# One SwiGLU up step by plain block products, a fixed TensorE order at its entry, row norms on VectorE and deeper lookahead

## The chip, the cores and the metric

The kernel runs on one core of one Trainium2 chip. The metric is the device time of one execution in microseconds (us); smaller is better. All arithmetic is fp32. A matrix product of fp32 operands is made of three TensorE matmuls on "fp32r" halves: every operand is split into a high part (h) and a low part (l = x - h), and h·h, h·l and l·h are summed in PSUM.

## The reference, cut to what matters

One layer: a token mixer (attention beside a gated MLP), then the SwiGLU feed-forward part, each followed by a layer norm of the scaled residual. The change lies in the second half:

```
z   = layer_norm(alpha*x + g1 * mixer(x)) * ln1_g + ln1_b     # (1024, 1024)
h2  = z * (1 + scale) + shift                                 # adaLN modulation
a   = silu(h2 @ w1) * (h2 @ w3)                               # w1, w3: (1024, 2816)
out = layer_norm(alpha*z + g2 * (a @ w2)) * ln2_g + ln2_b     # w2: (2816, 1024)
```

## The kernel before, in words

Z holds the eight 128-row tiles of the normalised stream, h2 its modulated transpose. The first half (mixer, output projection, h2 of the rows 512 to 1023) is not touched by the diff beyond line numbers.

**Up.** `h2 @ w1` and `h2 @ w3` are done in 22 steps (p, w): p is one of 11 pairs of 128 columns of the feed-forward width, w=0 is w1 and w=1 is w3. In each step a 2x2 block product is made with 7 block products in place of 8 (a Strassen-Winograd scheme), 12 matmuls of 128x512 each (`prod`, L1093 to L1095). `up_first` makes A11·B11 (PSUM tile pa, copied to SBUF at L1138), `up_second` adds A12·B21 on pa. `up_rest` makes S2·T2 (tile pb, added to the copy at L1153), S1·T1 and S4·B22 (first half "c" of tile pcd), S3·T3 and A22·T4 (second half "d" of pcd). c is copied by ScalarE (L1161), added by GpSimd (L1165), and d and c are added by VectorE (L1169, L1174, L1177). The S are sums of weight blocks (`prep2`, L1070 to L1078, then split), the T are sums of h2 blocks made once by `make_h2b`: eight groups of four TensorE transposes of Z (tile pz, written by L128), an affine on ScalarE (L845, tiles h2X and h2H), subtractions and splits on VectorE. A split is a cast on ScalarE (L102, wH) and a subtraction on VectorE (L107, wL). `act_out` does the silu on ScalarE (w=0) and the product on VectorE (w=1, L1115) and sends activations to a DRAM tile combP. `w2_sums(p)` loads a block of w2, scales it on GpSimd (L1035), forms four sums on VectorE (tile wt) and sends these to combP too. Of the first NE=5 steps `up_first` and `up_second` run ahead, while the T are not there yet; they need B11 and B21 alone.

**Down.** `a @ w2` takes the products P1, P5, P6, P3, P2, P7, P4 in that order, each over the 11 p, 12 matmuls for each (L1292, PSUM tiles px and py). Operands are read back from combP (tile cr) and split (L102, L107) `prep_to` pairs ahead of TensorE. Between products VectorE adds PSUM to the rows R (L1239, L1365). Rows 4 to 7 are complete after P2 and are normalised by `norm_slow` while P7 runs: statistics (L1259, L1261, L123), the root on GpSimd (L124, L1268), scale on ScalarE (L1270), gain on VectorE (L1272), bias on GpSimd (L1274). Rows 0 to 3 are completed by P4 and go through `norm_fast` (L1282, L1284).

**Order.** Every engine runs its instructions in the order in which they stand. A recording layer fixes this order when the program is built, from the order of the code and its estimates; `order(a, b)` forces a behind b, and `at` puts a VectorE instruction behind the last recorded matmul. Dependencies are kept for whole tiles: the two halves of pcd count as one.

## Time and profile before

| | us |
|---|---|
| median of 3 runs (1256.88 to 1259.43) | 1257.02 |
| the profiled execution's own time | 1260.01 |
| its span in the profile | 1258.3 |
| TensorE (PE) busy | 1201.2 (95%) |
| VectorE (DVE) busy | 960.7 (76%) |
| ScalarE (ACT) busy | 563.3 (45%) |
| GpSimd (POOL) busy | 324.9 (26%) |

The span is the profiled stretch of that one execution; its own time includes 1.7 us around the span. Busy shares are means over stages: TensorE is at 95% over all, but stretches with gaps stand between stretches without any. The mean granted TensorE clock of the execution is 0.986 of full speed.

### The profile page before, as it was taken

Reading aid. Unit: us, or ns where it says so; the run is one execution under the profiler, and the core shown is the slowest. Engines: PE = TensorE matmul, PEld = TensorE weight load, DVE = VectorE, ACT = ScalarE, POOL = GpSimd, SP = SyncE. Lnnn points to the kernel's source line nnn. Section 1 sums busy time; section 2 is a strip of 40 time slices with the busy share of each in tenths; the row PEclk is TensorE's granted clock in tenths of the full one; section 3 lists DMA queues with packets and bytes.
Section 4 is the critical chain, followed back from the end, with each engine's and each line's share of the span. In section 5 each row is a group of like instructions: output and inputs, shape, how many; then the busy total and the mean of one; then the engine's idle time right before and its main releaser. Section 6 shows DMA issues by size and latency. Waiting matters only on the chain.

```text
span 1258.3 us, 16864 instructions
## 1 busy us (share of the span) xinstructions
PE 1201.2 (95%) x5884; PEld 998.5 (79%) x5884; DVE 960.7 (76%) x1682; ACT 563.3 (45%) x1033; POOL 324.9 (26%) x331
## 2 busy tenths in 40 slices
PE   7999999999999999999788999999999999999977
PEld 5888888788888888788566878888888877888865
DVE  6568798699999988776877766866767769864685
ACT  5644223499889993134412331332322323552440
POOL 0022045266456753100223202222122200000131
PEclk9999999999999999999889989999999999999989
DMA  9624549010000006542156655456565569893552
GB/s 355 232 67 122 169 138 239 28 68 1 1 2 1 2 19 234 184 131 96 47 179 209 192 164 173 157 184 192 170 190 177 160 224 347 274 302 106 194 181 83
DMA packets 131979, 188.60 MB, mean 150 GB/s; under 512 B 16819, under 2 KB 78387, under 8 KB 131894
## 3 DMA queue, kind: packets, MB, share of 16 engines
q1 hardware_dynamic: 131894, 187.52, 46.1%
q8 instruction: 46, 0.75, 0.3%
q14 instruction: 39, 0.32, 0.1%
HBM read 136.63 MB, written 48.76 MB: 147 GB/s over the span
## 4 chain that ended last, share of the span: by engine, by line
PE 79%; DVE 11%; DMA 4%; issue 3%; ACT 2%; POOL 1%; DVEq 0%; SPq 0%; ACTq 0%; POOLq 0%
PE py L1292 7%; PE px L1292 6%; PE pcd L1093 5%; PE pcd L1094 5%; PE pcd L1095 5%; PE pt L128 4%; PE pa L1093 3%; PE pa L1095 3%; PE pa L1094 3%; PE ps L730 2%; PE ps L732 2%; PE ot L774 2%; PE pwo L92 2%; PE pwo L96 2%; PE pwo L95 2%
## 5 line engine op out<-in xcount | busy, mean ns | idle before, releaser
L102 ACT ACTIVATE wH<-cr 128x1024 fp32r<-128x1024 f32 x77 | 80.8, 1059 | 104.7 <-DMA cr<-combP 95.1
L743 POOL TENSOR_SCALAR P<-P,ast,gate 128x640 f32<-128x640 f32 (+7 forms) x128 | 99.5, 783 | 66.5 <-DVE ast L742 42.2
L107 DVE TENSOR_TENSOR wL<-cr,wH 128x1024 fp32r<-128x1024 f32 x77 | 100.3, 1317 | 20.0 <-ACT wH L102 19.1
L1165 POOL TENSOR_TENSOR pt<-pt,pt 128x512 f32<-128x512 f32 x22 | 36.3, 1648 | 269.9 <-DVE pt L1153 181.4
L107 DVE TENSOR_TENSOR pt<-pt,pt 128x512 fp32r<-128x512 f32 (+1 forms) x148 | 99.9, 682 | 7.0 <-ACT pt L102 6.3
L676 ACT ACTIVATE P<-P,ast 128x640 f32<-128x640 f32 (+7 forms) x128 | 94.0, 736 | 2.0 <-DVE ast L675 1.5
L102 ACT ACTIVATE pt<-pt 128x512 fp32r<-128x512 f32 (+1 forms) x148 | 87.4, 593 | 16.1 <-PE pt L128 13.4
L1035 POOL TENSOR_TENSOR w2r<-w2r,g2r 128x512 f32<-128x512 f32 x44 | 62.8, 1448 | 72.0 <-DMA w2r<-in_w 60.4
L128 PE MATMUL pt<-ident,P 128*128 128x128 f32 x528 | 79.0, 272 | 0.2 <-DVE pt L107 0.2
L1292 PE MATMUL px<-wH 128*128 128x512 f32 x176 | 68.5, 396 | 9.1 <-DVE r L1239 6.8
L102 ACT ACTIVATE wH<-raw 128x1024 fp32r<-128x1024 f32 (+2 forms) x41 | 42.4, 1040 | 76.2 <-DMA combP<-wt 63.3
L128 PEld LDWEIGHTS pt<-ident,P 128*128 128x128 f32 x528 | 65.0, 140 | 12.9 <-issue 0.5
L1093 PE MATMUL pa<-h2H,wH 128*128 128x512 f32 x176 | 70.2, 400 | 4.2 <-ACT wH L102 3.5
L1095 PE MATMUL pa<-h2H,wL 128*128 128x512 f32 x176 | 69.6, 395 | 1.8 <-DVE wL L107 1.8
L1093 PE MATMUL pcd<-wH,wH 128*128 128x512 f32 x176 | 70.1, 398 | 1.1 <-ACT wH L102 0.7
L107 DVE TENSOR_TENSOR wL<-raw,wH 128x1024 fp32r<-128x1024 f32 (+2 forms) x41 | 49.0, 1198 | 28.6 <-ACT wH L102 22.9
L1094 PE MATMUL pcd<-wL,wH 128*128 128x512 f32 x176 | 69.8, 397 | 0.6 <-DVE wL L107 0.6
L1292 PE MATMUL px<-wL,wH 128*128 128x512 f32 x176 | 69.1, 393 | 1.0 <-DVE wL L107 1.0
L1094 PE MATMUL pa<-h2L,wH 128*128 128x512 f32 x176 | 69.9, 397 | 0.0
L1095 PE MATMUL pcd<-wH,wL 128*128 128x512 f32 x176 | 69.2, 393 | 0.0
L1292 PE MATMUL px<-wH,wL 128*128 128x512 f32 x176 | 69.0, 392 | 0.0
L773 PE MATMUL ot<-pt,V 128*128 128x512 f32 x132 | 59.7, 452 | 0.0
(298 smaller groups left out, 3500.8 us busy)
## 6 DMA issues: line engine op xcount, KB each, us to landing
cr<-combP SPq DMA_DIRECT2D x77, 512.0 KB, 4.8
raw<-in_w SPq DMA_DIRECT2D x49, 512.0 KB, 6.0
ada<-in_w_adaT SPq DMA_DIRECT2D x32, 512.0 KB, 6.8
w2r<-in_w SPq DMA_DIRECT2D x44, 256.0 KB, 3.0
combP<-wt SPq DMA_DIRECT2D x44, 256.0 KB, 5.5
combP<-as SPq DMA_DIRECT2D x44, 256.0 KB, 2.1
combP<-w2r SPq DMA_DIRECT2D x33, 256.0 KB, 2.0
ada<-in_w_ada SPq DMA_DIRECT2D x32, 256.0 KB, 3.7
```

Of the source, the lines that this page charges most:

```text
L102: A_.activation(o, i, AF.Copy)
L107: return V_.tensor_tensor(o, i, f(h), SUB)
L128: nc.tensor.transpose(out=p[:, j * 128:(j + 1) * 128], in_=src(j), identity=ident)
L676: A_.activation(P, P, AF.Exp, scale=-1.0, bias=nm, accum_out=den)
L743: P_.tensor_scalar(P, P, st[:, 2, hh:hh + 1], gcol(i, h, br), MULT, MULT)
L773: nc.tensor.matmul(ot, vs, hl[0], start=False, stop=False)
L1035: order(P_.tensor_tensor(r[z][a], r[z][a], rowt["g2r"][:, a * 512:a * 512 + 512], MULT), lasth[0])
L1093: nc.tensor.matmul(o, lh, rh, start=start and i == 0, stop=False, skip_group_check=not start)
L1094: nc.tensor.matmul(o, lh, rl, start=False, stop=False, skip_group_check=not start)
L1095: r = nc.tensor.matmul(o, ll, rh, start=False, stop=i == 3, skip_group_check=not start)
L1165: P_.tensor_tensor(p5, p5, p1, ADD)
L1292: lastm[0] = nc.tensor.matmul(o, x_[:, ts_], y_[:, 512:1024], start=not cont and p == 0 and n == 0, stop=p == NP - 1 and n == 2, skip_grou ...
```

## The change

1. The first up step (p=0, both w) is made by 8 plain block products in place of 7 (`classic`): A11·B11 + A12·B21 and its three sisters. It takes no S and no T, but a split B12, which `make_h2b` makes with B22. Two of the four plain outputs go on pa ahead of the T, the other two (on the halves of a pcd tile) after the two early `up_first`/`up_second` of the steps 2 and 3. NE becomes 4.
2. All early products and the transposes of Z are chained in their order of the code (`in_order`); a part of `make_h2b` is issued after the 13th, 16th, 19th and 22nd group of three matmuls (`TR`).
3. T1 to T4 are formed later and in another order, and the tie `lasth` that held `w2_sums` behind them is gone.
4. `w2_sums` of p=0, 1, 2 runs at the steps 3, 5, 4 and no longer at 0, 2, 4.
5. `up_rest` has one order for all steps (S4·B22 after S3·T3).
6. `norm_slow` has two VectorE instructions (subtract the mean and multiply by the gain; multiply by the root and add the bias) in place of the chain over GpSimd, ScalarE, VectorE and GpSimd.
7. `prep_to` looks up to 7 further pairs ahead from n=24 on, in place of up to 4 from n=40 on.

```diff
...
     def make_h2b():
 
         x12, x22, x11, x21 = [], [], X1P[0:2], X1P[2:4]
+
+        def place(n, j, t):
+            h, l = split(t)
+            BOP[n][2 * j:2 * j + 2] = zip(halves(h), halves(l))
         for i in range(4):
             if i % 2 == 0:
                 x12.append(B("h2X"))
...
                 bh, bl = B("h2H", F32R), B("h2L", F32R)
             for k, xx in ((i, x12[-1]), (4 + i, x22[-1])):
                 p = S2("pz")[:, 0, :]
-                trans4(p, lambda j: Z[j][:, k * 128:(k + 1) * 128])
+                for j in range(4):
+                    in_order(nc.tensor.transpose(out=p[:, j * 128:(j + 1) * 128], in_=Z[j][:, k * 128:(k + 1) * 128], identity=ident))
                 affine("A", halves(xx)[i % 2], p, k)
                 if k >= 4:
                     affine("A", halves(bh)[i % 2], p, k)
             if i % 2:
                 sub(bl, x22[-1], bh)
                 BOP["B22"][i - 1:i + 1] = zip(halves(bh), halves(bl))
-                t1 = x11[i // 2]
-                V_.tensor_tensor(t1, x12[-1], t1, SUB)
-                h, l = split(t1)
-                BOP["T1"][i - 1:i + 1] = zip(halves(h), halves(l))
+                place("B12", i // 2, x12[-1])
             yield
         spill_z(0)
-
-        def place(n, j, t):
-            h, l = split(t)
-            lasth[:] = lasts
-            BOP[n][2 * j:2 * j + 2] = zip(halves(h), halves(l))
         for j in range(2):
+            V_.tensor_tensor(x11[j], x12[j], x11[j], SUB)
+            place("T1", j, x11[j])
             V_.tensor_tensor(x11[j], x22[j], x11[j], SUB)
-            V_.tensor_tensor(x21[j], x21[j], x11[j], SUB)
             place("T2", j, x11[j])
             yield
         for j in range(2):
             V_.tensor_tensor(x12[j], x22[j], x12[j], SUB)
             place("T3", j, x12[j])
-            yield
-        for j in range(2):
+            V_.tensor_tensor(x21[j], x21[j], x11[j], SUB)
             place("T4", j, x21[j])
             yield
+
+    lastpe = []
+
+    def in_order(i):
+
+        if lastpe:
+            order(i, lastpe[0])
+        lastpe[:] = [i]
+        return i
 
     def advance_h2(n=1):
         for _ in range(n):
...
             load(r[z][0], w2[(2 * p + z) * 128:(2 * p + z + 1) * 128, 0:512], 8)
             load(r[z][1], w2[(2 * p + z) * 128:(2 * p + z + 1) * 128, 512:1024], 8)
             for a in range(2):
-                order(P_.tensor_tensor(r[z][a], r[z][a], rowt["g2r"][:, a * 512:a * 512 + 512], MULT), lasth[0])
+                P_.tensor_tensor(r[z][a], r[z][a], rowt["g2r"][:, a * 512:a * 512 + 512], MULT)
         (t1, t3), (t2, t4) = halves(B("wt")), halves(B("wt"))
         V_.tensor_tensor(t1, b12, b11, SUB)
         V_.tensor_tensor(t3, b22, b12, SUB)
...
         sub(l, a22, h)
         o["A22"] = pieces(h, l)
 
-    def prod(o, a, b, start=True):
+    ticks = [0]
+
+    def prod(o, a, b, start=True, early=False):
 
         for i in range(4):
             (lh, ll), (rh, rl) = a[i], b[i]
-            nc.tensor.matmul(o, lh, rh, start=start and i == 0, stop=False, skip_group_check=not start)
-            nc.tensor.matmul(o, lh, rl, start=False, stop=False, skip_group_check=not start)
-            r = nc.tensor.matmul(o, ll, rh, start=False, stop=i == 3, skip_group_check=not start)
+            for n, (x_, y_) in enumerate(((lh, rh), (lh, rl), (ll, rh))):
+                r = nc.tensor.matmul(o, x_, y_, start=start and i == 0 and n == 0, stop=i == 3 and n == 2, skip_group_check=not start)
+                if early:
+                    in_order(r)
+            if early:
+                ticks[0] += 1
+                if ticks[0] in TR:
+                    advance_h2()
         marks.append(r)
 
     early_acts = []
 
     def room(p, q):
 
-        if q or (p, 0) not in steps[:NE]:
+        if not (p == 0 and q in (0, 2) or p == 1 and q == 0):
             return H2()
         if not early_acts:
             early_acts.extend(halves(B("ea")))
...
                 V_.tensor_tensor(s2, s1, a[0], SUB)
                 for i, t in (("P5", s1), ("P6", s2), ("P7", s3)):
                     put(i, p, 0, t)
-            if q == 2:
+            if q in (1, 2) and 2 in a and "s" in a:
                 _, (s2, s4) = a["s"]
                 V_.tensor_tensor(s4, a[2], s2, SUB)
                 put("P3", p, 0, s4)
 
-    def up_first(p, w):
+    def up_first(p, w, early=False):
 
         o = ops[p, w]
         a = G("pa")
-        prod(a, o["A11"], BOP["B11"])
+        prod(a, o["A11"], BOP["B11"], True, early)
         p1 = keep[p, w] = H2(F32, "pt")
         A_.activation(p1, a, AF.Copy)
         return a
 
-    def up_second(p, w, a):
-        prod(a, ops[p, w]["A12"], BOP["B21"], False)
+    def up_second(p, w, a, early=False):
+        prod(a, ops[p, w]["A12"], BOP["B21"], False, early)
         act_out(p, w, 0, a)
 
-    def up_rest(p, w, a, c_first=False):
+    def classic(w, q, o, early=False):
+
+        r, c = str(q // 2 + 1), str(q % 2 + 1)
+        prod(o, ops[0, w]["A" + r + "1"], BOP["B1" + c], True, early)
+        prod(o, ops[0, w]["A" + r + "2"], BOP["B2" + c], False, early)
+        act_out(0, w, q, o)
+
+    def up_rest(p, w, a):
         o, p1 = ops[p, w], keep.pop((p, w))
         b = (OT if (2 * p + w) % 2 else G)("pb")
         cd = S2("pcd")
         c, d = cd[:, 0, :], cd[:, 1, :]
-
-        def second():
-            prod(b, o["S2"], BOP["T2"])
-            V_.tensor_tensor(p1, p1, b, ADD)
-
-        def third():
-            prod(c, o["S4"], BOP["B22"], False)
-        if not c_first:
-            second()
+        prod(b, o["S2"], BOP["T2"])
+        V_.tensor_tensor(p1, p1, b, ADD)
         prod(c, o["S1"], BOP["T1"])
         p5 = H2(F32, "pt")
         A_.activation(p5, c, AF.Copy)
-        if c_first:
-            third()
-            second()
         P_.tensor_tensor(p5, p5, p1, ADD)
         if a is not None:
             up_second(p, w, a)
         prod(d, o["S3"], BOP["T3"])
         V_.tensor_tensor(p5, p5, d, ADD)
         act_out(p, w, 3, p5)
-        if not c_first:
-            third()
+        prod(c, o["S4"], BOP["B22"], False)
         p7 = H2(F32, "pt")
         V_.tensor_tensor(p7, p1, c, ADD)
         act_out(p, w, 1, p7)
...
         act_out(p, w, 2, p1)
 
     steps = [(p, w) for p in range(NP) for w in range(2)]
-    NE = 5
-    for n in range(NE):
+    NE, TR = 4, (13, 16, 19, 22)
+
+    def prep_classic(w):
+        for z in range(2):
+            h, l = split(load_w((w1, w3)[w], z))
+            ops.setdefault((0, w), {}).update({f"A{z + 1}1": pieces(h, l), f"A{z + 1}2": pieces(h, l, 512)})
+    prep_classic(0)
+    prep_classic(1)
+    for n in (2, 3):
         prep1(*steps[n])
-    prep2(*steps[0], lastz)
-    for n in range(NE):
-        up_second(*steps[n], up_first(*steps[n]))
-        if n == 1:
-            advance_h2(4)
+    for w in range(2):
+        for q in (0, 2):
+            classic(w, q, G("pa"), True)
+    for n in (2, 3):
+        up_second(*steps[n], up_first(*steps[n], True), True)
     advance_h2(100)
-    prep2(*steps[1], lasth[0])
+    prep2(*steps[2])
+    for w in range(2):
+        cd = S2("pcd")
+        for q in (3, 1):
+            classic(w, q, cd[:, q // 2, :])
     seq2 = [(i, p) for i in DN for p in range(NP)]
     ops2 = {}
 
...
     def down_start():
         prep_to(3)
 
+    W2 = {3: 0, 4: 2, 5: 1}
     for n, s in enumerate(steps):
-        if 1 < n + 1 < len(steps):
+        if n < 2:
+            continue
+        if n + 1 < len(steps):
             if n + 1 >= NE:
                 prep1(*steps[n + 1])
             prep2(*steps[n + 1])
-        if s[1] == 0:
-            w2_sums(s[0])
+        if n in W2 or n > 5 and s[1] == 0:
+            w2_sums(W2.get(n, s[0]))
         if n == len(steps) - 1:
             down_start()
-        up_rest(*s, up_first(*s) if n >= NE else None, n == 0)
+        up_rest(*s, up_first(*s) if n >= NE else None)
 
 
     R = [B("r") for _ in range(NT)]
...
     def norm_slow(t):
         mv = stats(t, 0)
         yield
-        P_.tensor_scalar(mv[:, 3:4], mv[:, 0:1], mv[:, 2:3], -1.0, MULT, MULT)
         z = B("zo")
-        at(A_.activation(z, R[t], AF.Identity, scale=mv[:, 2:3], bias=mv[:, 3:4]))
+        at(V_.scalar_tensor_tensor(z, R[t], mv[:, 0:1], l2[0], SUB, MULT))
         yield
-        at(V_.tensor_tensor(z, z, l2[0], MULT))
-        yield
-        at(P_.tensor_tensor(z, z, l2[1], ADD))
+        at(V_.scalar_tensor_tensor(z, z, mv[:, 2:3], l2[1], MULT, ADD))
         dma(out[t * 128:(t + 1) * 128], z)
         yield
 
...
     for t in range(8):
         later(residual((4 + t) % 8))
     for n, (i, p) in enumerate(seq2):
-        prep_to(n + LA2 + max(0, min(4, (n - 40) // 6)))
+        prep_to(n + LA2 + max(0, min(7, (n - 24) // 4)))
         if p == 0:
             cont = i not in ("P1", "P5", "P2")
             if i == "P1":
```

TensorE at the entry of the up stage (pa is the tile of an early product, named by its number; h2H/h2L are parts of h2, wH/wL of a weight block; pz takes transposes of z). Before, the first transposes stand behind 59 matmuls of early products:

```order
L1094 MATMUL pa_6342<-h2L_6057,wH_6270 128x512
L1095 MATMUL pa_6342<-h2H_6056,wL_6271 128x512
L1094 MATMUL pa_6443<-h2L_5925,wH_6276 128x512
L128 MATMUL pz_6375<-ident,z_6015 128x128
L128 MATMUL pz_6375<-ident,z_6013 128x128
L128 MATMUL pz_6375<-ident,z_5897 128x128
```

In the changed kernel they stand behind 39 matmuls, in a chain that holds every one of these rows in its place:

```order
L1102 MATMUL pa_6325<-h2H_6025,wH_6270 128x512
L1102 MATMUL pa_6325<-h2L_6026,wH_6270 128x512
L1102 MATMUL pa_6325<-h2H_6025,wL_6271 128x512
L880 MATMUL pz_6345<-ident,z_6015 128x128
L880 MATMUL pz_6345<-ident,z_6013 128x128
L880 MATMUL pz_6345<-ident,z_5897 128x128
```

The transposes have moved up by 20 matmuls, and the product on pa_6325 is cut in two by them.

VectorE, where the last T splits stand before (wL from h2X is a T split, sa is the first S sum of the next step, L1153, L1169 and L1174 are the additions of the first `up_rest`):

```order
L107 TENSOR_TENSOR wL_6542<-h2X_5926,wH_6541 128x1024
L107 TENSOR_TENSOR wL_6547<-h2X_6371,wH_6546 128x1024
L107 TENSOR_TENSOR wL_6552<-h2X_6407,wH_6551 128x1024
L1153 TENSOR_TENSOR pt_6326<-pt_6326,pb_6607 128x512
L107 TENSOR_TENSOR wL_6556<-h2X_6027,wH_6555 128x1024
L107 TENSOR_TENSOR wL_6560<-h2X_6058,wH_6559 128x1024
L1070 TENSOR_TENSOR sa_6567<-raw_6563 128x512
L1169 TENSOR_TENSOR pt_6621<-pt_6621,pcd_6608 128x512
L1073 TENSOR_TENSOR sa_6567<-sa_6567,raw_6565 128x512
L1174 TENSOR_TENSOR pt_6664<-pt_6326,pcd_6608 128x512
```

and in the changed kernel (L1128 is `act_out`'s product, first of the plain outputs; sa is the S sum of step 2):

```order
L107 TENSOR_TENSOR wL_6554<-h2X_5926,wH_6553 128x1024
L107 TENSOR_TENSOR wL_6559<-h2X_6341,wH_6558 128x1024
L107 TENSOR_TENSOR wL_6564<-h2X_6027,wH_6563 128x1024
L107 TENSOR_TENSOR wL_6569<-h2X_6396,wH_6568 128x1024
L1128 TENSOR_TENSOR h_6623<-h_6623,pcd_6651 128x512
L107 TENSOR_TENSOR wL_6574<-h2X_6058,wH_6573 128x1024
L1076 TENSOR_TENSOR sa_6581<-raw_6577 128x512
L1079 TENSOR_TENSOR sa_6581<-sa_6581,raw_6579 128x512
L107 TENSOR_TENSOR wL_6586<-sa_6581,wH_6585 128x1024
L1081 TENSOR_TENSOR sb_6582<-raw_6579,raw_6577 128x512
```

Before, additions that free pb and pcd stand between and behind the T splits; now there are plain outputs' products between them and no addition of an `up_rest` before the S sums of step 2.

VectorE at the end of product P7 (px holds P7's sums, the four additions on r from px free it for P4; wL from cr is the split of an operand of P4, l a row of gains or biases). Before:

```order
L123 TENSOR_SCALAR stb_9621<-stb_9621 128x1
L1272 TENSOR_TENSOR zo_10903<-zo_10903,l_10460 128x1024
L107 TENSOR_TENSOR wL_10908<-cr_10905,wH_10907 128x1024
L107 TENSOR_TENSOR wL_10931<-cr_10928,wH_10930 128x1024
L107 TENSOR_TENSOR wL_10951<-cr_10948,wH_10950 128x1024
L1239 TENSOR_TENSOR r_9607<-r_9607,px_9630 128x512
L1239 TENSOR_TENSOR r_9608<-r_9608,px_9630 128x512
L107 TENSOR_TENSOR wL_10973<-cr_10970,wH_10972 128x1024
L1239 TENSOR_TENSOR r_9609<-r_9609,px_9631 128x512
```

In the changed kernel:

```order
L123 TENSOR_SCALAR stb_9601<-stb_9601 128x1
L1292 SCALAR_TENSOR_TENSOR zo_10922<-r_9594,stb_9601,l_10464 128x1024
L107 TENSOR_TENSOR wL_10931<-cr_10928,wH_10930 128x1024
L1262 TENSOR_TENSOR r_9587<-r_9587,px_9610 128x512
L1262 TENSOR_TENSOR r_9588<-r_9588,px_9610 128x512
L1262 TENSOR_TENSOR r_9589<-r_9589,px_9611 128x512
L1262 TENSOR_TENSOR r_9590<-r_9590,px_9611 128x512
L1294 SCALAR_TENSOR_TENSOR zo_10922<-zo_10922,stb_9601,l_10466 128x1024
```

Three splits stand between the last gain and the additions before, one instead of them now; the second norm instruction of the last row stands behind the additions.

## Rows read from the trace of the kernel before

**Rows 1.** The page: busy time, VectorE's tenths in 40 slices, shares of the last chain.

```profile
PE 1201.2 (95%) x5884; PEld 998.5 (79%) x5884; DVE 960.7 (76%) x1682; ACT 563.3 (45%) x1033; POOL 324.9 (26%) x331
...
DVE  6568798699999988776877766866767769864685
...
PE 79%; DVE 11%; DMA 4%; issue 3%; ACT 2%; POOL 1%; DVEq 0%; SPq 0%; ACTq 0%; POOLq 0%
```

**Rows 2.** Windows: stretch and length, then busy us (instructions) by engine, PEclk.

```profile
620.00:640.00 20.00, 13.12 (x43) 10.33 (x44) 15.37 (x19) 5.96 (x8) 5.87 (x4) 0.76 0.64 197
...
780.00:1020.00 240.00, 239.64 (x1057) 197.75 (x1056) 171.92 (x225) 75.95 (x105) 53.29 (x37) 1.00 0.59 187
...
1200.00:1220.00 20.00, 13.22 (x52) 10.53 (x51) 17.59 (x19) 7.74 (x8) 5.08 (x4) 0.83 0.61 209
```

**Rows 3.** Waits of PE, 570 to 780: us in total, times, longest.

```profile
PE pb L1093 <- ACT wH L102: 8.3, 3, 4.6
...
PE pcd L1093 <- DVE pt L1174: 5.6, 1, 5.6
...
PE pa L1093 <- ACT wH L102: 3.1, 1, 3.1
...
PE pa L1095 <- DVE wL L107: 1.8, 1, 1.8
```

**Rows 4.** Timeline, PE: start, length, instruction, [idle before it <- releaser].

```profile
570.05 0.39 PE L1093 MATMUL pa<-h2H,wH 128*128 128x512 f32 x1
...
570.27 0.39 PE L1094 MATMUL pa<-h2L,wH 128*128 128x512 f32 x1
...
583.43 1.03 PE L128 MATMUL pz<-ident,z 128*128 128x128 f32 x8
...
584.22 0.48 PE L1095 MATMUL pa<-h2H,wL 128*128 128x512 f32 x1
...
622.31 0.79 PE L1093 MATMUL pcd<-wH,w 128*128 128x512 f32 x1 [5.59 <-DVE pt L1174]
...
622.90 0.63 PE L1094 MATMUL pcd<-wL,w 128*128 128x512 f32 x1
...
623.33 0.63 PE L1095 MATMUL pcd<-wH,w 128*128 128x512 f32 x1
...
637.12 0.80 PE L1093 MATMUL pb<-wH,wH 128*128 128x512 f32 x1 [4.57 <-ACT wH L102]
...
743.21 0.79 PE L1093 MATMUL pa<-h2H,wH 128*128 128x512 f32 x1 [3.11 <-ACT wH L102]
...
1021.59 0.39 PE L1292 MATMUL px<-wH 128*128 128x512 f32 x1
```

**Rows 5.** Timeline, DVE, entry of the up stage.

```profile
577.18 1.70 DVE L1014 TENSOR_SCALAR z<-z,mv 128x1024 f32<-128x1024 f32 x2 [0.58 <-POOL mv L124]
...
610.73 3.49 DVE L107 TENSOR_TENSOR wL<-h2X,wH 128x1024 fp32r<-128x1024 f32 x3
...
614.87 3.44 DVE L107 TENSOR_TENSOR wL<-h2X,wH 128x1024 fp32r<-128x1024 f32 x2
...
621.58 0.68 DVE L1174 TENSOR_TENSOR pt<-pt,pcd 128x512 f32<-128x512 f32 x1
```

**Rows 6.** Timeline, POOL, the first `w2_sums`.

```profile
617.19 6.84 POOL L1035 TENSOR_TENSOR w2r<-w2r,g2r 128x512 f32<-128x512 f32 x4
```

**Rows 7.** Timeline, ACT, just before PE resumes at 743.21.

```profile
742.10 1.06 ACT L102 ACTIVATE wH<-raw 128x1024 fp32r<-128x1024 f32 x1 [8.57 <-DMA combP<-wt]
```

**Rows 8.** Timeline, PE, first matmul of P4.

```profile
1216.89 0.77 PE L1292 MATMUL px<-wH 128*128 128x512 f32 x1 [6.78 <-DVE r L1239]
```

**Rows 9.** Timeline, DVE and POOL, end of P7.

```profile
1209.92 5.64 DVE L107 TENSOR_TENSOR wL<-cr,wH 128x1024 fp32r<-128x1024 f32 x3
...
1210.15 3.19 POOL L1274 TENSOR_TENSOR zo<-zo,l 128x1024 f32<-128x1024 f32 x1 [2.69 <-PE px L1292]
```

**Rows 10.** Groups, DVE, 1225 to the end: `norm_fast`'s first instruction.

```profile
L1282 DVE SCALAR_TENSOR_TENSOR zo<-r,stb,l 128x1024 f32<-128x1024 f32 x3 | 3.8, 1274 | 0.0
```

More of the change, by code (lines that the diff above doesn't have):

```diff
@@ L833, in hymba_kernel @@
     zspill = dram.tile([NT, 128, 1024], F32, name="zspill")
-    X1P, BOP = [], {n: [None] * 4 for n in ("B11", "B21", "B22", "T1", "T2", "T3", "T4")}
+    X1P, BOP = [], {n: [None] * 4 for n in ("B11", "B21", "B12", "B22", "T1", "T2", "T3", "T4")}
     def halves(t):
```

## The prediction, made before the changed kernel had run

> **What bounds the kernel now.** I read the page first. TensorE is busy for 95% of the span and holds 79% of the last chain [rows 1], so time can only be won where TensorE waits or runs slowly, or lost where it gets more matmuls. Then the windows [rows 2]: from 780 to 1020, in the steady up steps, TensorE is busy for 239.64 of 240 us at full clock; nothing is to be had there. At 620 to 640 it is busy for 13.12 of 20 us with PEclk 0.76, at 1200 to 1220 for 13.22 of 20 us with 0.83. The reader is to see two holes, one at the entry of the up stage and one where P7 gives way to P4. The waits of TensorE [rows 3] and its timeline [rows 4] name them: 8.3 us in three waits for a cast of a split (the longest 4.57 at 637), 5.59 us for the addition L1174 at 622, 3.11 us for a cast at 743, 1.8 us for a split; and at 1216.89 a wait of 6.78 us for an addition on r [rows 8].
>
> The up stage as a sum. 59 matmuls stand between 570.05 and 583.43, so one takes 0.2268 us at full clock; eight transposes take 0.79 us (583.43 to 584.22); at half clock a matmul takes 0.43 us (622.90 to 623.33) [rows 4]. From the first early product at 570.05 to the first matmul of the down stage at 1021.59 are 451.5 us [rows 4]. The work in them is 22 x 7 x 12 = 1848 matmuls, 419.1 us, and 32 transposes, 3.2 us. **29.2 us are lost.** The waits shown make 18.8 of it; shorter waits and matmuls at half clock are the other 10.4. So one us of a wait costs about 1.55 us in all, and I price long waits so.
>
> Why the holes are there. L1174 ran at 621.58, behind eight splits of the T and half an S sum that stand ahead of it on VectorE (third and fourth fence of the change); the next product writes the other half of pcd, and the two halves count as one tile. Two T splits of 3.44 us took 1.72 each, against 1.16 for the three at 610.73 [rows 5], since GpSimd scaled w2 from 617.19 for 6.84 us [rows 6] and added before that. So VectorE is what the entry waits for. In P7 three splits took 5.64 us, not 3.48, beside GpSimd's bias addition of 3.19 us [rows 9], and VectorE came 6.78 us late to the additions that free px.
>
> **The change part by part.**
>
> Plain products: the two steps of p=0 go from 14 to 16 block products, 24 matmuls more: 24 x 0.2268 = **+5.4 us**, on the path for certain. They also take S sums and splits of two steps and all additions of two `up_rest` from VectorE, and add two splits of B12, 1.16 us each there and 1.06 each on ScalarE [rows 5, 7]; these lie behind the 39 matmuls and ahead of the T, with some 200 matmuls of early products as cover; without it they would cost 4.4 us.
>
> Fixed order: the transposes stand behind 39 matmuls, and 570.05 + 39 x 0.2268 = 578.9. The last z is ready at 577.18 + 1.70 = 578.9 [rows 5]. I take 0 for this wait (below nothing it cannot go, since nothing can be put in its place; 1.2 us at most: one more weight split of 1.16 us now stands ahead of z's last steps on VectorE, and if the wait for the output projection's last matmuls doesn't cover it, z is late by it and all is).
>
> The T: the first product with a T now comes behind 240 matmuls and 32 transposes, at 570.05 + 54.4 + 3.2 + about 0.8 for one wait (below) = 628.5. The T casts on ScalarE stand behind the silu of step 2's early output, which waits for the 142nd matmul, at about 605.5. From there VectorE has eight splits, four subtractions of the same size, two output products at 0.68, the first S sum and, behind its cast, its split: 9.3 + 4.6 + 1.4 + 1.4 + 1.06 + 1.16 = 18.9 us, and some handovers; ready at 625 to 628. I take no wait.
>
> What waits remain or come. (a) The plain output on one half of pcd waits for VectorE's product on the other: one operation of 0.68 [rows 5] and the handover, 0.8. (b) S3·T3 behind ScalarE's copy of the other half, likewise 0.7. (c) Step 3's S2 split, 1.0; between 0 and what the same split of step 1 cost, 4.57 x 1.55 = 7.1 [rows 4]. (d) VectorE's additions behind the sums of `w2_sums` at step 3, 1.5; between 0 and the 1.8 of [rows 3]. (e) A weight cast of step 6 still stands behind the landing of a w2 sum in combP, as the cast at 742.10 did, when ScalarE had idled 8.57 us [rows 7]: 2.0; between 0 and 3.11 x 1.55 = 4.8. (f) Short ones later, 2.2. Together **8.2 us**: low end 3, high end 0.8 + 0.7 + 7.1 + 1.8 + 4.8 + 2.2 = 17.4. I sit nearer to the low end, as (c) has half of its VectorE work taken away. Up stage: 5.4 - 29.2 + 8.2 = **-15.6 us**.
>
> `norm_slow`: four times ScalarE's scale, VectorE's gain and GpSimd's bias go, and two VectorE instructions of 1.27 us [rows 10] come. P7 is 132 matmuls, 29.9 us; its px is complete in the first half 6 matmuls earlier, at 28.6. Ahead of the additions VectorE has, in P7: four additions of py, 2.7; four sets of statistics of about 1.0; seven of the new instructions, 8.9; ten splits (fourteen before), 11.6: 27.2 us. It is there by 28.6; two additions of 0.68 later P4 starts, 0.3 late. Lookahead moves four splits into P3 and P2, where VectorE's slices are at 4 to 6 tenths (36th to 38th digit) [rows 1], and their loads too; cost nothing, with half the engine as cover. The hole at 1216.89 cost 6.78 plus half clock: 20 us hold 13.22/0.2268 = 58 matmuls at full clock by busy time, 52 are there [rows 2], so 1.4 more. **8.2 - 0.3 = -7.9 us**; bounds 0 and 8.2.
>
> The regrouped `w2_sums` and `up_rest`'s one order add no matmul; their price is in (b), (d) and (e).
>
> Sum: -15.6 - 7.9 = **-23.5 us**. The profiled execution took 1260.0, 3.0 above the median of the runs; I take the same difference off both: 1236.5 for it, and **1233.5 as the median**.
>
> One rule weighs against (4). The windows of the steady steps first: VectorE 171.92 and GpSimd 53.29 of 240 us [rows 2], per step of 84 matmuls (19.05 us) 13.6 and 4.2. Beside GpSimd, splits lost 1.1 of 3.44 us [rows 5] or 2.2 of 3.19 [rows 9], some half. So VectorE's own work is about 11.5 a step; every second step has `w2_sums`, four half operations on VectorE and 6.84 us on GpSimd [rows 6], so 12.7 and 7.6 in such a step. 12.7 and half of 7.6 are 16.5 of 19.05: it fits, three times in a row as well. The Trainium skill ("SBUF — State Buffer", Who interferes with whom) has GpSimd and VectorE share one port pair as an exclusive lock, the loser fully blocked, two-input VectorE instructions included. By that page of the Trainium skill a step with `w2_sums` would be 12.7 + 7.6 = 20.3 us, 1.25 over, three such steps in a row 3.8 us late, and the median 1237.3 in place of 1233.5. The trace agrees in kind, but shows half of GpSimd's time lost and not all.
>
> **The rivals.**
>
> Waits come back at steps 2 to 8 (17%): (c) to (e) at their high ends, as the T work is late or the three `w2_sums` in a row fill VectorE, GpSimd and the queue of loads. For it: the T come with 1 to 3 us to spare, and the loads and stores of three sums fall within three steps. Against: VectorE's removed work. 1233.5 + 9.2 = 1242.7. Of the 17, 5 are for VectorE held as long as GpSimd runs, 1.25 us over in three steps, 3.8 in all: 1237.3.
>
> The tail hole stays (7%): VectorE is 1.4 us ahead by the sum; a row's output DMA that holds a zo buffer, or a load that comes late, puts it behind. 1233.5 + 7.9 = 1241.4. Against: no GpSimd addition beside it any more.
>
> Hardly any wait remains (10%): 8.2 becomes 3: 1228.3.
>
> The fixed order loses more than the change wins (4%): at each of the four `TR` points TensorE may do nothing else while pz is still being read by ScalarE's three affines (half tiles; 0.7 each as an estimate, between half and the whole of the cast's 1.06 [rows 7]). From one such point to the next are 9 matmuls and 8 transposes, 2.8 us, and ScalarE is nearly full with 2.1 and the casts. From 6.5 us of wait at each of the four it decides (26 us); with each as long as the wait at 622, 5.59 x 1.55 = 8.7, 1233.5 + 34.7 = 1268. Against: two pz groups stand apart, and z is ready in time.
>
> The plain products do not shorten the entry's waits and only cost (2%): 1257.0 + 5.4 - 7.9 = 1254.5.
>
> **How the numbers follow.** My forecast has 60%, 1229 to 1239 by (c) to (f) in part. The range of 8 in 10 runs from 1226, below the case with hardly any wait, to 1245, above those of returned waits and of the tail. Differences under 0.2% (2.5 us) a measurement here can hardly tell from no change. Faster by more than that are all cases but the last two: 0.94; the last one is the same, 0.02; the fixed order's is slower, 0.04.
>
> **What would show it.** Right: the first transposes at 578.9 without a wait; the first T product near 628; no wait over 3 us between 620 and 780, PEclk 0.95 or more there; the first px matmul at about 1006; P4's first matmul under 1 us after P7's last; 5908 matmul records. Wrong: waits at the four transposes' places, a wait of more than 4 us for a T or S split, a long wait for DVE's additions at P4, or new waits in P5 to P2 behind loads taken too early.

## The result, and the profile after

The changed kernel takes **1242.68 us** (median of 4 runs, 1242.14 to 1243.80) against 1256.95 us before (4 runs, 1256.48 to 1259.43): ratio 0.9884, 95% interval [0.9867, 0.9901]. On another occasion it was 1244.28 against 1256.07, 0.9904 [0.9890, 0.9918]. So it is faster by 1.0 to 1.2%, 12 to 14 us. The range of 1226 to 1245 holds the time; the likeliest case, 1233.5, was 9 us too low, and the number is that of the rival in which waits come back.

The profiled execution took 1242.14 us, its span is 1240.4. First the page: TensorE, and the shares of the last chain, which answer to [rows 1].

```profile
PE 1199.7 (97%) x5908; PEld 998.2 (80%) x5908; DVE 951.4 (77%) x1668; ACT 555.6 (45%) x1023; POOL 313.7 (25%) x321
...
PE 86%; DVE 8%; issue 2%; DMA 2%; ACT 1%; POOL 0%; DVEq 0%; SPq 0%; ACTq 0%; POOLq 0%
```

TensorE has 24 records more, as it should, and its share of the chain went from 79 to 86%, DVE's from 11 to 8. Next the windows, with the columns of [rows 2].

```profile
620.00:640.00 20.00, 18.53 (x81) 14.71 (x80) 15.43 (x21) 6.91 (x8) 2.52 (x1) 1.00 0.37 118
...
660.00:680.00 20.00, 18.25 (x79) 14.15 (x78) 18.76 (x21) 3.79 (x5) 7.82 (x5) 1.00 0.69 238
...
680.00:700.00 20.00, 16.09 (x64) 12.76 (x64) 15.31 (x18) 5.36 (x9) 7.59 (x5) 0.91 0.65 224
...
720.00:740.00 20.00, 15.82 (x62) 12.16 (x61) 13.89 (x20) 6.78 (x9) 1.61 (x1) 0.91 0.62 184
...
800.00:1000.00 200.00, 200.00 (x885) 165.58 (x884) 146.45 (x193) 61.27 (x84) 42.22 (x30) 1.00 0.57 181
...
1180.00:1200.00 20.00, 20.00 (x90) 16.43 (x88) 15.64 (x19) 5.31 (x5) 3.27 (x3) 1.00 0.45 158
```

The hole at 620 to 640 is closed (18.53 of 20 us at full clock, against 13.12), and the end of P7 is solid (20.00 at 1180 to 1200; P4 starts at 1200.35, see below). Two new holes stand at 680 to 700 and 720 to 740, with PEclk 0.91. The waits of TensorE in the whole up stage name them (us in total, times, longest; compare [rows 3]):

```profile
PE pa L1102 <- ACT wH L102: 7.9, 2, 4.0
PE pb L1102 <- DVE wL L107: 1.8, 2, 1.6
PE pcd L1102 <- DVE h L1128: 0.8, 1, 0.8
PE pcd L1102 <- ACT pt L1174: 0.7, 1, 0.7
```

11.2 us are left; over the same stage of the kernel before it was 21.8, of which [rows 3] show 18.8. The timeline of TensorE shows where (as in [rows 4]):

```profile
571.09 0.39 PE L1102 MATMUL pa<-h2H,wH 128*128 128x512 f32 x1
...
579.97 1.09 PE L880 MATMUL pz<-ident,z 128*128 128x128 f32 x8
...
624.68 0.50 PE L1102 MATMUL pcd<-wH,wH 128*128 128x512 f32 x1 [0.78 <-DVE h L1128]
...
630.25 0.39 PE L1102 MATMUL pb<-wH,wH 128*128 128x512 f32 x1
...
678.34 0.50 PE L1102 MATMUL pb<-wH,wL 128*128 128x512 f32 x1 [1.64 <-DVE wL L107]
...
689.82 0.73 PE L1102 MATMUL pa<-h2H,wH 128*128 128x512 f32 x1 [3.91 <-ACT wH L102]
...
734.68 0.79 PE L1102 MATMUL pa<-h2H,wH 128*128 128x512 f32 x1 [4.01 <-ACT wH L102]
...
1011.10 0.39 PE L1312 MATMUL px<-wH 128*128 128x512 f32 x1
```

From 571.09 to 1011.10 the up stage takes 440.0 us, against 451.5: -11.5. The first early product comes 1.0 us later; in the fourteen profiles of this study, whose mixer is the same code, it lies between 569.9 and 573.0. From the first px to the end of the span are 229.3 us, against 236.7: -7.4. -11.5 - 7.4 + 1.0 is the difference of the spans, 17.9. 24 matmuls of the up stage, 5.4 us, stand behind the first px, in both kernels alike. That leaves the measured difference as it is, but 34.6 us were lost in this stage before, not 29.2, and 440.0 - 1848 x 0.2268 - 3.2 = 17.7 after.

What holds the cast ahead of 689.82 (SyncE's queue, VectorE and ScalarE, in order of time, then the cast at the same place two steps later):

```profile
679.57 0.38 SPq L86 DMA_DIRECT2D raw<-in_w  x1
...
682.97 0.69 DVE L1044 TENSOR_TENSOR wt<-w2r,w2r 128x512 f32<-128x512 f32 x1
...
683.08 0.92 SPq L1033 DMA_DIRECT2D combP<-wt  x2
...
688.71 1.06 ACT L102 ACTIVATE wH<-raw 128x1024 fp32r<-128x1024 f32 x1 [7.08 <-DMA combP<-wt]
...
733.58 1.06 ACT L102 ACTIVATE wH<-raw 128x1024 fp32r<-128x1024 f32 x1 [7.11 <-DMA combP<-wt]
```

VectorE forms two sums in the halves of a wt tile until 683.7; their stores are issued at 683.1 and 683.7 and have landed at 688.0 and 688.6; ScalarE has then been idle for 7.08 us and the cast can write. The weight block it casts has nothing to do with that store: its own load, issued at 679.57, had landed 4.8 us later, at 684.3. The cast writes into the buffer of the wt tile. Tiles of this size come from one pool of 41 buffers, and the one that this cast gets is the one just stored. The cast at 733.58 stands in the same way behind the stores of the sums of p=3 at step 6, which the change does not move. By the count of matmuls (636 ahead of the product that waits for it, 612 plus the 24 more in the kernel before) it is the cast that cost 3.11 us at 743.21 [rows 4]. The one at 688.71 is new as a wait: it stands behind the sums of step 4.

The end of P7 (VectorE, then TensorE):

```profile
1198.92 1.28 DVE L1262 TENSOR_TENSOR r<-r,px 128x512 f32<-128x512 f32 x2 [4.06 <-PE px L1312]
...
1199.85 0.39 PE L1312 MATMUL px<-wH,wL 128*128 128x512 f32 x1
...
1200.35 0.47 PE L1312 MATMUL px<-wH 128*128 128x512 f32 x1
```

VectorE waits 4.06 us for px, where before px waited for it; P4's first matmul stands 0.50 us behind P7's last, 0.27 more than the pace.

### The profile page after: what moved, and what is told of

It reads as the page before. It is cut to its first block, busy times and chain, and to the rows that moved or that the text cites. A ratio compares the mean times of both kernels' runs of the same rounds, so it can differ in the third digit from the quotient of the medians.

```text
span 1240.4 us, 16864 instructions
## 1 busy us (share of the span) xinstructions
PE 1199.7 (97%) x5908; PEld 998.2 (80%) x5908; DVE 951.4 (77%) x1668; ACT 555.6 (45%) x1023; POOL 313.7 (25%) x321
## 4 chain that ended last, share of the span: by engine, by line
PE 86%; DVE 8%; issue 2%; DMA 2%; ACT 1%; POOL 0%; DVEq 0%; SPq 0%; ACTq 0%; POOLq 0%
PE pcd L1102 17%; PE pa L1102 10%; PE px L1312 8%; PE py L1312 7%; PE pt L128 4%; PE pb L1102 4%; PE ps L730 2%; PE ps L732 2%; PE pwo L92 2%; PE pwo L95 2%; PE pwo L96 2%; PE ot L774 2%; PE ot L773 2%; PE pv L92 1%; PE pv L95 1%
## 5 line engine op out<-in xcount | busy, mean ns | idle before, releaser
L107 DVE TENSOR_TENSOR wL<-cr,wH 128x1024 fp32r<-128x1024 f32 x77 | 93.9, 1233 | 25.3 <-ACT wH L102 24.9
L1175 POOL TENSOR_TENSOR pt<-pt,pt 128x512 f32<-128x512 f32 x20 | 32.0, 1598 | 241.6 <-DVE pt L1171 147.7
L1102 PE MATMUL pa<-h2H,wH 128*128 128x512 f32 x192 | 76.9, 401 | 7.9 <-ACT wH L102 7.9
L107 DVE TENSOR_TENSOR wL<-raw,wH 128x1024 fp32r<-128x1024 f32 (+2 forms) x43 | 55.4, 1291 | 31.2 <-ACT wH L102 29.3
L1102 PE MATMUL pa<-h2L,wH 128*128 128x512 f32 x192 | 76.1, 396 | 0.0
L1102 PE MATMUL pa<-h2H,wL 128*128 128x512 f32 x192 | 75.6, 394 | 0.0
L124 POOL TENSOR_TENSOR stb<-stb,mhalf 128x1 f32<-128x1 f32 x8 | 11.6, 1447 | 193.7 <-DVE stb L123 193.7
```

Source lines behind the costliest of these rows:

```text
L107: return V_.tensor_tensor(o, i, f(h), SUB)
L1102: r = nc.tensor.matmul(o, x_, y_, start=start and i == 0 and n == 0, stop=i == 3 and n == 2, skip_group_check=not start)
L1175: P_.tensor_tensor(p5, p5, p1, ADD)
```

## The experiments

Stages are taken from each profile: "up" from the first early product to the first px matmul, "down" from there to the end of the span. Differences below 3 us between profiles of one stage are not to be trusted: the same up stage took 451.5, 450.4, 450.1 and 448.2 us in the four profiles that contain it unchanged. A profile is of one execution, which here lies up to 3.8 us from its kernel's median.

| kernel | time, median us | before beside it | ratio, 95% | up | down |
|---|---|---|---|---|---|
| before | 1256.95 | | | 451.5 | 236.7 |
| changed | 1242.68 | 1256.95 | 0.9884 [0.9867, 0.9901] | 440.0 | 229.3 |
| b_norm | 1249.36 | 1257.88 | 0.9934 [0.9920, 0.9948] | 450.4 | 228.0 |
| b_look | 1253.68 | 1257.88 | 0.9969 [0.9954, 0.9983] | 450.1 | 232.9 |
| b_tail | 1248.91 | 1257.88 | 0.9929 [0.9917, 0.9941] | 448.2 | 227.9 |
| b_w2 | 1252.90 | 1257.88 | 0.9958 [0.9944, 0.9972] | 442.4 | 236.0 |
| a_wt1 | 1238.87 | 1258.56 | 0.9843 [0.9822, 0.9864] | 436.1 | 228.8 |
| a_spread | 1239.51 | 1258.56 | 0.9847 [0.9829, 0.9866] | 438.9 | 228.4 |
| a_free | 1240.76 | 1258.56 | 0.9866 [0.9844, 0.9889] | 439.8 | 228.1 |
| a_notail | 1251.02 | 1258.56 | 0.9938 [0.9921, 0.9955] | 439.2 | 237.8 |
| a_again | 1244.28 | 1256.07 | 0.9904 [0.9890, 0.9918] | 442.1 | 231.2 |
| b_w2tail | 1243.97 | 1256.07 | 0.9905 [0.9891, 0.9919] | 443.3 | 228.0 |
| a_best | 1236.37 | 1256.07 | 0.9833 [0.9819, 0.9846] | 434.3 | 228.6 |
| b_best | 1240.52 | 1256.07 | 0.9876 [0.9862, 0.9889] | 439.6 | 228.2 |

**The tail, part by part.** b_norm puts the new `norm_slow` (the hunk of the diff shown above) into the kernel before; b_look only the line

```diff
-        prep_to(n + LA2 + max(0, min(4, (n - 40) // 6)))
+        prep_to(n + LA2 + max(0, min(7, (n - 24) // 4)))
```

and b_tail both.

> The kernel before with the two VectorE instructions in norm_slow alone (lookahead as before). Theory that VectorE's amount of work in P7 sets the hole: 14 splits, 16.2 us, are left beside 8.9 us of new instructions, so VectorE is about 3 us late in place of 6.8, and the time falls by 3.5 to 5 us. Rival, that GpSimd's bias addition and the idle time for ScalarE were the hole: P4 starts less than 1 us late and the time falls by 7.5 us.

> The kernel before with the deeper lookahead alone (norm_slow as before). Theory of the amount of work: four splits less in P7, two of them stretched, take 5 to 6 us off the wait of 6.8, so the time falls by 5 to 7 us. Rival, that the chain ScalarE, VectorE, GpSimd sets it: the wait stays above 4 us and the time falls by less than 3 us.

> The kernel before with both tail edits, the up stage untouched. Theory: the hole at P4 closes (wait under 1 us), 7.9 us less. Rival, that the tail is worth less by itself: under 5 us.

`norm_slow` alone gave 8.5 us, and no wait is left at P4. The end of P7 on VectorE in b_norm:

```profile
1206.73 2.36 DVE L107 TENSOR_TENSOR wL<-cr,wH 128x1024 fp32r<-128x1024 f32 x2
...
1209.95 1.28 DVE L1239 TENSOR_TENSOR r<-r,px 128x512 f32<-128x512 f32 x2 [0.87 <-PE px L1289]
...
1211.15 1.22 DVE L107 TENSOR_TENSOR wL<-cr,wH 128x1024 fp32r<-128x1024 f32 x1
```

VectorE reaches the additions 0.87 us before px is complete. Thirteen splits stand ahead of them, not fourteen, and VectorE had begun with py at 1179.4, 2 us before P7, since py is complete bank by bank: 3 us that my count had too much. So the rival (GpSimd's addition and the idle time of the old chain are the hole) holds; no run tells these two apart. b_look alone:

```profile
1199.56 5.68 DVE L107 TENSOR_TENSOR wL<-cr,wH 128x1024 fp32r<-128x1024 f32 x3
...
1209.53 1.23 DVE L107 TENSOR_TENSOR wL<-cr,wH 128x1024 fp32r<-128x1024 f32 x1 [3.25 <-ACT wH L102]
...
1214.37 0.77 PE L1292 MATMUL px<-wH 128*128 128x512 f32 x1 [3.29 <-DVE r L1239]
```

Three splits still take 5.68 us beside GpSimd, VectorE idles 3.25 us, and P4 waits 3.29 us: of 6.78 us half is gone, 4.2 us in time. That is between its two expectations. Together they give 9.0 us, not more than `norm_slow` alone; lookahead only adds margin (VectorE waits 4.31 us for px in b_tail, against 0.87 in b_norm). The term of 7.9 us is right in size; it belongs to `norm_slow`.

**The sums of w2 alone.** b_w2 is the kernel before with

```diff
-        if s[1] == 0:
-            w2_sums(s[0])
+        W2 = {3: 0, 4: 2, 5: 1}
+        if n in W2 or n > 5 and s[1] == 0:
+            w2_sums(W2.get(n, s[0]))
```

> The kernel before with w2_sums of p=0, 2, 1 at the steps 3, 4, 5 alone. Theory that the T come too late whatever GpSimd does: the waits at the entry shrink only by what the splits lost beside GpSimd, 1 to 2 us, and the time falls by 2 to 4 us. Rival, that GpSimd and the w2 loads at the entry cause the waits: 10 us or more less. Third: with the sums crowded in three steps, later waits take the gain, no change.

The up stage fell to 442.4 us, by some 8, the time by 5.0 (the profiled execution was the fastest of six, 2.7 us under their median). The waits of TensorE that are left there and are worth a line:

```profile
620.96 0.79 PE L1093 MATMUL pcd<-wH,w 128*128 128x512 f32 x1 [4.23 <-DVE pt L1174]
...
672.30 0.50 PE L1093 MATMUL pcd<-wH,w 128*128 128x512 f32 x1 [0.83 <-DVE pt L1174]
...
706.57 0.50 PE L1093 MATMUL pcd<-h2H,wH 128*128 128x512 f32 x1 [1.72 <-DVE pt L1169]
...
735.01 0.50 PE L1093 MATMUL pcd<-wH,w 128*128 128x512 f32 x1 [1.86 <-DVE pt L1174]
```

5.59 us at 622 became 4.23 at 621; the waits of 4.57 (637), 2.78 (673) and 3.11 (743) are gone, and shorter ones of 0.8 to 1.9 came. So the T were late in any case, as I had it, but the three long waits behind them came from the sums that stood at the steps 0 and 2. In size it lies between the first theory and its rival.

**The other half of that question**, b_w2tail: the line above and the two tail edits in the kernel before, so without plain products, fixed order and new order of the T.

> The changed kernel again, beside the next three on one chip. All theories: as at first, 14 to 16 us less than before; the waits of 3.9 and 4.0 us at a step's first cast are there again.

> The kernel before with the moved w2_sums and the two tail edits: the change without the plain products, the fixed order and the new order of the T. If the moved sums carry the up stage (442.4 us from the first early product to the first of the down stage in the run with them alone, 440.0 in the changed kernel): within 3 us of the changed kernel. Rival, that the plain products' time for the T is what pays: 7 us or more above the changed kernel.

The changed kernel is 11.8 us under the kernel before this time, not 14 to 16, and its two waits are there again, at 3.63 and 4.88 us. b_w2tail takes 1243.97 beside its 1244.28 us: no difference, as the first theory had it. The plain products with their order buy as much as their 24 matmuls cost, no more. This is the main finding: **what the changed kernel gains in the up stage, the moved sums gain without the rest.** The reverse, the plain products with the sums as early as they can stand, did not run; so it isn't shown that the moved sums are needed beside the plain products.

**The tail taken out of the changed kernel**, a_notail (both hunks undone):

> The changed kernel with norm_slow and lookahead as before. Theory that the two holes don't depend on each other: the wait of about 6.8 us at P4 is back and the time is 7 to 8.5 us above the changed kernel, some 6 to 7 us under the kernel before.

```profile
1204.74 0.76 PE L1315 MATMUL px<-wH 128*128 128x512 f32 x1 [6.79 <-DVE r L1262]
```

The wait is back at 6.79 us, down takes 237.8 us, and the kernel is at 1251.0, by medians 7 to 8 us above the changed one, by the ratios to the kernel before 4 to 7 (the two ran on different occasions, as did the next three). Within that the two holes don't depend on each other.

**The fixed order**, a_free:

```diff
     def in_order(i):
-
-        if lastpe:
-            order(i, lastpe[0])
-        lastpe[:] = [i]
         return i
```

> The changed kernel without the chain that fixes TensorE's order at the entry (the recording layer then puts the first transposes behind 59 matmuls and spreads them over 60 more). Theory that the T casts are held by ScalarE's queue until about 605 anyway: within 1.5 us of the changed kernel. Rival, that the early transposes make the T ready in time: T up to 10 us later, waits at the first T products, 5 us or more slower.

439.8 us of up stage, 1240.8 us: not slower, as the theory had it; that it is 2 to 4 us faster by medians can't be told, since its interval overlaps the first one of the changed kernel. A reason that fits is in the changed kernel's own trace on VectorE:

```profile
608.75 1.23 DVE L107 TENSOR_TENSOR wL<-h2X,wH 128x1024 fp32r<-128x1024 f32 x1 [11.32 <-ACT wH L102]
...
618.20 4.82 DVE L107 TENSOR_TENSOR wL<-h2X,wH 128x1024 fp32r<-128x1024 f32 x4
...
628.28 1.23 DVE L107 TENSOR_TENSOR wL<-sa,wH 128x1024 fp32r<-128x1024 f32 x1 [1.19 <-ACT wH L102]
```

The first split of a T waits 11.32 us for its cast, which stands behind a silu on ScalarE; the first transposes come 4 us earlier in the fixed order (579.97 against 584.4 in a_free), and their T wait there. The first T product comes 59.2 us behind the first product with the fixed order and 58.1 without it.

**The two waits for wt.** a_wt1 needs one new tile in place of two:

```diff
-        (t1, t3), (t2, t4) = halves(B("wt")), halves(B("wt"))
+        (t1, t2), t3, t4 = halves(B("wt")), b12, b11
+        for i, b in (("P1", b11), ("P2", b21), ("P3", b22)):
+            put(i, p, 1, b)
...
-        for i, b in zip(("P1", "P2", "P3", "P4", "P5", "P6", "P7"), (b11, b21, b22, t4, t1, t2, t3)):
+        for i, b in (("P4", t4), ("P5", t1), ("P6", t2), ("P7", t3)):
```

> The changed kernel with one new tile in place of two in w2_sums: t3 and t4 are written over b12 and b11 after these are stored, same instructions. Theory that the casts at 688.7 and 733.6 wait since their buffer was a wt tile whose store has not landed: both waits of TensorE fall to 1.5 us or less and the time falls by 5 to 9 us. Rival, that the raw weight block itself lands late: waits stay above 3 us, no change. Second rival: the w2 tiles are held longer, new waits of the same size.

Both waits are gone. The same cast as at 688.71 in a_wt1 (ScalarE), and the longest wait left near it (TensorE):

```profile
687.49 1.06 ACT L102 ACTIVATE wH<-raw 128x1024 fp32r<-128x1024 f32 x1 [3.19 <-DMA raw<-in_w]
...
680.96 0.79 PE L1104 MATMUL pb<-wH,wL 128*128 128x512 f32 x1 [1.61 <-DVE wL L107]
```

TensorE does not wait for the cast any more; up takes 436.1 us, 4 to 6 less. The row names the load of the cast's own block, but that was issued at 682.19 and landed 4.4 us later, at 686.6: ScalarE was held until 687.42, when the store of an `as` tile, issued at 682.97, had landed, so the next buffer of the pool is a stored one too. The gain lies at the second cast. The first waiting product (468 matmuls ahead of it) comes 118.3 us behind the first product, against 118.7 in the changed kernel with its wait, since waits of 1.18 and 1.61 us just before it and matmuls at half clock took as much; the second (636 ahead) comes at 159.4 against 163.6. The medians are 4 to 5 us under the changed kernel's, the ratios to the kernel before 5 to 8: the low end of the theory's 5 to 9.

a_spread has `W2 = {3: 0, 5: 1, 7: 2}` in place of `{3: 0, 4: 2, 5: 1}`.

> The changed kernel with w2_sums of p=0, 1, 2 at the steps 3, 5, 7 (then 6, 8, ... for the others). Theory of the reused wt buffer: no sum at step 4, so the wait of 3.91 us at 689.8 goes, that at 734.7 stays; 3 to 5.5 us less. Rival, that three sums in three steps in a row cost wherever they are: waits of the same size move to steps 7 and 8, within 1 us of no change.

```profile
724.47 0.50 PE L1102 MATMUL pa<-h2H,wH 128*128 128x512 f32 x1 [3.46 <-ACT wH L102]
...
769.73 0.80 PE L1102 MATMUL pa<-h2H,wH 128*128 128x512 f32 x1 [4.36 <-ACT wH L102]
```

The wait at 689.8 is gone and the one at 734.7 is there, now at 724.5, as the theory had it; but one of 4.36 us has come at 769.7, two steps behind the latter, as its rival had it. In both kernels the sums stand in four steps in a row, since p=3 keeps step 6: 3 to 6 in the changed kernel, 5 to 8 here (GpSimd's scaling starts at 645, 667, 689 and 710 us there and at 677, 700, 724 and 744 here). The waits stand behind the second and the fourth of the four. By medians it is 3 to 5 us faster, by the profiles' up stage 1 to 3; how much of the rest is the occasion stays open.

**All of it together.** a_best is a_wt1, a_spread and a_free in one; b_best is b_tail with the sums at 3, 5, 7 and one tile (7 products in every step).

> The changed kernel without the fixed order, with w2_sums at 3, 5, 7 and with one new tile in place of two in it. If the gains of the three runs add: the up stage at 433 to 435 us, 4 to 6 us under the changed kernel. Rival, that the one-tile form alone had removed all that can be removed: 3 to 4 us under it.

> The kernel before with both tail edits, w2_sums at 3, 5, 7 and one new tile in place of two: 7 block products in every step. If the plain products buy 2 to 3 us net: 2 to 3 us above the kernel with them. Rival: with the sums out of the way and 24 matmuls fewer, it is as fast or faster.

a_best takes **1236.37 us**, 7.9 less than the changed kernel beside it, more than both forecasts, and 1.7% less than before; up is at 434.3 us. The longest waits of TensorE in its up stage:

```profile
PE pcd L1101 <- DVE pt L1185: 3.1, 2, 2.5
PE pa L1101 <- ACT pt L1150: 2.0, 1, 2.0
PE pb L1101 <- DVE wL L107: 0.7, 2, 0.6
```

b_best takes 1240.52, 4.2 us more than a_best. Here, with the buffers out of the way, the plain products and the order that comes with them are worth some 4 us net, more than the 2 to 3 forecast; in the changed kernel their cost of 5.4 us took all that they won.

## Why the prediction was right in range and wrong in its middle

**The base.** I took the profiled execution's 451.5 us of up stage as typical and the 3.0 us above the median as an offset. Three more profiles of the same stage gave 448.2 to 450.4, and the wait of 3.11 us at 743 was 2.14, 1.81 and 1.53 there: the landing of a store, which differs from run to run. The same store was in memory 6.3 us after its issue in the first profile and 5.4, 5.0 and 4.8 us after it in the others. So the base was 1 to 3 us too high.

**What the number owes to luck.** The sum -15.6 took all 1848 matmuls as standing ahead of the first px. With the 34.6 us that were lost in truth it would have been 5.4 us lower, the median 1228.1 and the miss 14.6 us. For what stays lost I had 8.2 us; 17.7 are. So more than half of the 9.5 us that the waits were priced too low was hidden by the miscount; a range moved with the sum would have ended at 1239.6 and not held the time. Of the 9.2 us of miss that show, 4.1 are the up stage, 1.0 its later start, 0.5 the tail and 3.5 the offset: the profiled execution was 3.0 us above its median before and 0.5 below it after.

**(e) and (f), the landing of the w2 sums.** This is the step that failed. "A weight cast of step 6 still stands behind the landing of a w2 sum in combP ...: 2.0" was right in place and cause and wrong in size: the cast behind the sums of step 6, ahead of 734.68, cost TensorE 4.01 us, and 1.8 more at half clock (15.82 us of busy time would hold 70 matmuls at 720 to 740, 62 are there). I had priced it at less than the 3.11 us that this very cast had cost before [rows 4]. The one two steps earlier, behind the sums of step 4, was at best part of (f), "short ones later, 2.2", and cost 3.91 and 1.6 (64 matmuls at 680 to 700, where 16.09 us would hold 71). Together 11.3 us in place of 4.2 at most. Nor do the sums stand "three times in a row": they stand so four times, at steps 3 to 6.

**(a) to (d).** 0.78 (forecast 0.8), 0.69 (0.7), nothing for step 3's split (1.0), 1.64 and 0.17 behind VectorE (1.5).

**Plain products, fixed order, T.** The 39 matmuls end at 579.97, 571.09 + 39 x 0.2268 = 579.94, no wait; the first T product comes at 630.25, 59.2 us behind the first product (forecast 58.4), no wait. So each step held as a step. But the sentence "So VectorE is what the entry waits for" led me to give the plain products, which relieve VectorE, what the moved sums did: b_w2tail has the same time without them. I priced the regrouped sums by their costs only, in (b), (d) and (e), and never what taking them out of steps 0 to 2 gives back.

**The tail.** -7.9 forecast, -7.4 in the profile, -9.0 in b_tail; P4 0.27 us late against 0.3. Of its two parts the lookahead is worth nothing that shows beside `norm_slow`.

**The rule on the shared port.** The first long wait follows the window in which, by the Trainium skill's lock ("SBUF — State Buffer", Who interferes with whom), VectorE would be over its time: it is busy for 18.76 of 20 us at 660 to 680. But a_wt1 runs the same VectorE instructions and has neither of the two long waits, so a full VectorE alone does not make them. I had put VectorE's loss at half of GpSimd's time, with GpSimd's stretched durations; my 1.1 of 3.44 us even set it against the splits' own duration. Here are two spots of the changed kernel, each with GpSimd first and VectorE beside it, and between them two GpSimd multiplications alone and a split alone.

```profile
645.39 3.91 POOL L1041 TENSOR_TENSOR w2r<-w2r,g2r 128x512 f32<-128x512 f32 x2 [6.31 <-DVE wL L107]
...
645.84 2.31 DVE L107 TENSOR_TENSOR wL<-raw,wH 128x1024 fp32r<-128x1024 f32 x1
...
648.08 1.78 DVE L1076 TENSOR_TENSOR sa<-raw 128x512 f32<-128x512 f32 x1
...
750.27 2.54 POOL L1041 TENSOR_TENSOR w2r<-w2r,g2r 128x512 f32<-128x512 f32 x2 [1.91 <-issue]
...
644.11 1.22 DVE L107 TENSOR_TENSOR wL<-sb,wH 128x1024 fp32r<-128x1024 f32 x1
...
713.02 3.49 POOL L1041 TENSOR_TENSOR w2r<-w2r,g2r 128x512 f32<-128x512 f32 x2 [0.64 <-DVE h L1128]
716.47 1.74 POOL L1175 TENSOR_TENSOR pt<-pt,pt 128x512 f32<-128x512 f32 x1
...
713.57 1.78 DVE L1136 TENSOR_TENSOR as<-h,h 128x512 f32<-128x512 f32 x1
715.27 1.78 DVE L1137 TENSOR_TENSOR as<-as,h 128x512 f32<-128x512 f32 x1
716.98 2.31 DVE L107 TENSOR_TENSOR wL<-raw,wH 128x1024 fp32r<-128x1024 f32 x1
```

Alone a GpSimd operation of this size takes 1.28 us, a split 1.22, and a VectorE operation of half a split, like L1076, L1136 or L1137, 0.68 (L1076 at 672.96). At the first spot VectorE takes 2.31 and 1.78 us for 1.22 and 0.68: it loses 2.2 us to 2.6 us of GpSimd's own work. At the second it takes 5.87 for 2.58 and loses 3.3 to 3.8. Both are 1.1 us for each GpSimd operation of 1.28, some 86%: near the lock and far from my half. Where VectorE's instruction had begun first, at 650.38, it took its 0.68 us, and GpSimd's, begun at 650.50, took 1.71. The step of mine that said a step with `w2_sums` takes 16.5 of 19.05 us was therefore too kind; by how much stays open, since not all of GpSimd's operations fall beside such an instruction.

The rivals: "waits come back" is what happened, by (e) and its twin, hardly by (c). The fixed order neither lost nor won. Of my own signs, these came true: no wait at the transposes, the place of the first T product, P4's start and the 5908 records. These did not: two waits stand over 3 us, PEclk is 0.91 in their windows, not 0.95 or more, and the first px comes at 1011.1, not 1006.

## What to carry to other kernels

Before a wait is given to the work that is late, move the other work that was put in the same place, alone: here one line of a table, with the tail edits, did what the whole rewritten first step did beside it. A tile that is stored by DMA keeps its buffer until the store has landed, and the next instruction to write into that buffer is the one that pays; look for an engine's idle time "released by" a transfer that its operands don't use. A profile is one draw: a term taken from a wait on a landing needs its spread from more than one execution.

## What the runs showed of the hardware

One and the same store landed 4.8 to 6.3 us after its issue in four executions of the same code, and the wait of TensorE behind it was 1.5 to 3.1 us. At the two spots above, a VectorE instruction with two inputs in SBUF that began after a GpSimd operation of 1.28 us took 1.1 us longer than alone, where I had counted on half.
